# Half of an output projection moved beside the attention, and probabilities flipped bank by bank

## The chip, the cores and the metric

The kernel runs on one core of one Trainium2 chip. The time is what the device takes for one execution, in microseconds (us); the figure of a kernel is the median over several runs. TensorE (PE in the profile) does the matrix products, VectorE (DVE), ScalarE (ACT) and GpSimd (POOL) the rest, SyncE (SP) issues the DMAs. Each engine works through its own instructions in a fixed order.

## The reference, cut to what matters

One Conformer-like block with D = 1024 and 512 positions, in float32:

```python
x = x + 0.5 * swiglu(rmsnorm(x, ffn1_norm), ffn1_w_gate, ffn1_w_up, ffn1_w_down)
proj = rmsnorm(x, mix_norm) @ w_in
out_a = chunked_relbias_attention(qa, ka, va, a_rel_bias)   # 8 heads of 64, chunks of 64, bias by distance
out_b = mla_attention(...)                                  # 8 heads of 96 (64 + 32 rotary), values of 64
x = x + jnp.concatenate([out_a, out_b], axis=-1) @ w_out
x = x + 0.5 * swiglu(rmsnorm(x, ffn2_norm), ffn2_w_gate, ffn2_w_up, ffn2_w_down)
x = rmsnorm(x, final_norm)
```

Both attentions are causal by blocks, so of the 4 x 4 blocks of 128 positions of a head only the ten on and below the diagonal are computed.

## The kernel before, in words

x stands transposed, as eight tiles `x[k]` of 128 features by 512 positions. Every matrix product is done in three passes on split numbers: a value is a rounded high part (a cast on ACT) and a low part (value minus high part, on DVE or POOL); `mm3` (L145 to L149) issues high x high (L147), the second pass L148 and the third L149. Weights come by `wunit` (L136 to L144): one DMA of 512 KB into one of four `raw` buffers, a cast to `whi` on ACT (L142), a subtraction to `wlo` on POOL (L143); `whi` and `wlo` have four buffers each.

The stages are: first feed-forward (gate and up products `gu`, down products `dn`), input projections and latents, 16 attention heads, output projection, second feed-forward, last norm. Heads 0 to 7 are those of A, heads 8 to 15 those of B. A loop over `it` from -2 to 16 (L569 to L578) lets four steps overlap: `flip(it)`, `softmax(it + 1)`, `front(it + 2)`, `values(it - 1)`.

- `front` turns queries and keys by TensorE transposes (tile `tr`, L457) and splits them on ACT (L461) and DVE (L462).
- `softmax` makes scores of four query blocks into `s3`, `s2` and the two halves of `s01`. Per block one DVE operation adds bias or mask and takes the row's minimum (L522, `mn`), ACT takes the exponential and the sum (L524), DVE the reciprocal (L525), POOL the product (L526). The probabilities lie in `pa` and `pb`, two of the four `raw` buffers.
- `flip` transposes the ten blocks of probabilities by TensorE (L542) into three PSUM banks `t0`, `t1`, `t2`, query block by query block, and copies them out as high parts on ACT (L547: PAh, PBh, in `whi` buffers) and low parts on DVE (L548: PAl, PBl, in `wlo` buffers).
- `values` multiplies with V into the bank `pv`; two heads share one, and after the second one ACT (L562) and DVE (L563) split it into AH[c], AL[c] (`xh`, `xl`), c = 0 to 3 for A and 4 to 7 for B.

The attention's eight PSUM banks are: 2 for `s`, 2 for `tr`, 3 for `t`, 1 for `pv`; in-projections before it use them in two groups of four (`bank`). The output projection (L589 to L599) then takes for each of eight tiles `dt` one `wunit` of `w_out[dt]`, 24 matmuls over c = 0 to 7 into one of seven banks of a new pool, adds the sum into `x[dt]` on DVE (L595) and prepares the second feed-forward: x2h on ACT (L596), x2l on DVE (L597), squares on ACT and their sum on POOL (`add_square`, L110).

The order in which an engine's instructions stand is not the source's: the framework's scheduler simulates the program's timing as it records it and sorts each engine's instructions by that. A tile that takes over a buffer waits for the last use of the buffer before.

## Time and profile before

| | us |
|---|---|
| median of 3 runs | 996.52 (996.40 to 996.64) |
| the profiled execution | 997.57 |
| its span | 995.8 |
| TensorE busy | 975.5 (98%) |
| POOL busy | 579.6 (58%) |
| ACT busy | 391.9 (39%) |
| DVE busy | 390.5 (39%) |
| attention up to the first `wo` matmul, starts at 482 | 579.30 |
| output projection up to the first second-stage `gu` matmul | 622.83 |

The last two rows are places on the span's clock. Busy times overlap; TensorE is the only engine that is busy nearly always. An idle engine other than it costs nothing by itself; an idle TensorE does, as no later stage is limited by anything else.

### The profile page before, as it was taken

The numbers are of one execution on the slowest core, as the hardware profiler recorded it, in microseconds if no ns is written. First come the engines' busy times: TensorE is split into PE (matmuls) and PEld (weight loads), VectorE is DVE, ScalarE is ACT, GpSimd is POOL, SyncE is SP. The second block draws the span as 40 slices with busy tenths as digits, with TensorE's granted clock in tenths as the row PEclk, the third lists the DMA queues.
The fourth block names the chain that finished last, engine by engine and source line by source line (L and its number), as shares of the span: only waits on it lengthen the run. The fifth ranks groups of instructions, "written<-read, shape, count | busy, mean of one in ns | idle before, by whom it ended". The sixth has DMA issues, their size and how long they took to land.

```text
span 995.8 us, 12076 instructions
## 1 busy us (share of the span) xinstructions
PE 975.5 (98%) x4579; PEld 812.1 (82%) x4579; DVE 390.5 (39%) x684; ACT 391.9 (39%) x661; POOL 579.6 (58%) x424
## 2 busy tenths in 40 slices
PE   9999999999999999898999999999999999999996
PEld 6888888888888889786778978888888888888886
DVE  7533333333121233866788845143333333200002
ACT  7533323232222236563778853343233232322321
POOL 4776666765555530385445567587666667645541
PEclk9999999999999999999999999999999999999998
DMA  6432223233233242220110062323322232333302
GB/s 233 145 109 86 102 89 106 85 106 95 83 102 93 89 141 75 85 64 1 32 33 2 1 212 88 103 86 106 102 88 99 93 104 80 101 96 95 101 16 85
DMA packets 29146, 89.90 MB, mean 90 GB/s; under 512 B 3488, under 2 KB 5664, under 8 KB 29088
## 3 DMA queue, kind: packets, MB, share of 16 engines
q1 hardware_dynamic: 28224, 88.34, 27.6%
q8 instruction: 36, 0.59, 0.2%
q10 hardware_dynamic: 864, 0.79, 0.2%
q14 instruction: 22, 0.18, 0.1%
HBM read 87.02 MB, written 2.10 MB: 89 GB/s over the span
## 4 chain that ended last, share of the span: by engine, by line
PE 89%; DVE 4%; ACT 3%; POOL 2%; issue 1%; DMA 1%; SPq 0%; POOLq 0%; ACTq 0%; DVEq 0%
PE gu L147 15%; PE gu L149 15%; PE gu L148 15%; PE dn L147 8%; PE dn L149 8%; PE dn L148 8%; PE pj L149 2%; PE pj L147 2%; PE pj L148 2%; PE wo L147 1%; PE wo L149 1%; PE wo L148 1%; PE t L542 1%; PE s L147 1%; PE tr L457 1%
## 5 line engine op out<-in xcount | busy, mean ns | idle before, releaser
L143 POOL TENSOR_TENSOR wlo<-raw,whi 128x1024 fp32r<-128x1024 f32 x138 | 324.2, 2350 | 153.3 <-ACT whi L142 152.5
L142 ACT CAST whi<-raw 128x1024 fp32r<-128x1024 f32 (+2 forms) x159 | 162.4, 1022 | 447.7 <-PE gu L148 244.8
L147 PE MATMUL gu<-x2h,whi 128*128 128x512 f32 x352 | 136.9, 389 | 0.0
L148 PE MATMUL gu<-x2l,whi 128*128 128x512 f32 x352 | 136.8, 389 | 0.0
L149 PE MATMUL gu<-x2h,wlo 128*128 128x512 f32 x352 | 136.8, 389 | 0.0
L148 PE MATMUL gu<-xl,whi 128*128 128x512 f32 x320 | 124.5, 389 | 0.0
L147 PE MATMUL gu<-xh,whi 128*128 128x512 f32 x320 | 124.5, 389 | 0.0
L149 PE MATMUL gu<-xh,wlo 128*128 128x512 f32 x320 | 124.5, 389 | 0.0
L162 POOL TENSOR_TENSOR us<-us,gs 128x512 f32<-128x512 f32 x44 | 57.6, 1310 | 108.7 <-DVE us L160 107.2
L161 DVE SCALAR_TENSOR_TENSOR gs<-th,gs 128x512 f32<-128x512 f32 x44 | 91.1, 2074 | 31.8 <-ACT th L159 31.8
L158 DVE TENSOR_TENSOR gs<-gu,rs 128x512 f32<-128x512 f32 x44 | 30.4, 691 | 175.9 <-PE gu L149 168.7
L191 DVE SCALAR_TENSOR_TENSOR x<-dn,x 128x512 f32<-128x512 f32 (+1 forms) x17 | 11.2, 660 | 193.9 <-PE dn L149 193.9
L148 PEld LDWEIGHTS gu<-x2l,whi 128*128 128x128 f32 x352 | 66.1, 188 | 13.8
L149 PEld LDWEIGHTS gu<-x2h,wlo 128*128 128x128 f32 x352 | 66.1, 188 | 13.8
L147 PEld LDWEIGHTS gu<-x2h,whi 128*128 128x128 f32 x352 | 66.1, 188 | 13.6
L149 PEld LDWEIGHTS gu<-xh,wlo 128*128 128x128 f32 x320 | 60.1, 188 | 12.6
L147 PEld LDWEIGHTS gu<-xh,whi 128*128 128x128 f32 x320 | 60.1, 188 | 12.5
L148 PEld LDWEIGHTS gu<-xl,whi 128*128 128x128 f32 x320 | 60.1, 188 | 12.3
L147 PE MATMUL dn<-h1h,whi 128*128 128x512 f32 x176 | 68.5, 389 | 0.0
L148 PE MATMUL dn<-h1l,whi 128*128 128x512 f32 x176 | 68.5, 389 | 0.0
L149 PE MATMUL dn<-h1h,wlo 128*128 128x512 f32 x176 | 68.5, 389 | 0.0
L160 DVE SCALAR_TENSOR_TENSOR us<-gu,rs 128x512 f32<-128x512 f32 x44 | 30.4, 690 | 64.9 <-PE gu L149 64.9
(327 smaller groups left out, 1864.5 us busy)
## 6 DMA issues: line engine op xcount, KB each, us to landing
raw<-in_gu SPq DMA_DIRECT2D x84, 512.0 KB, 3.6
raw<-in_dn SPq DMA_DIRECT2D x32, 512.0 KB, 3.5
raw<-in_dn SPq DMA_DIRECT2D x16, 384.0 KB, 3.1
raw<-in_w_in SPq DMA_DIRECT2D x12, 512.0 KB, 3.4
raw<-in_w_out SPq DMA_DIRECT2D x8, 512.0 KB, 4.3
x<-in_xT SPq DMA_DIRECT2D x8, 256.0 KB, 5.4
raw<-in_gu SPq DMA_DIRECT2D x8, 256.0 KB, 5.4
bias<-in_bias_tab SPq DMA_DIRECT2D x8, 256.0 KB, 2.7
```

Source lines behind the costliest of these rows:

```text
L142: act.copy(hi[:, :n], raw[:, :n])
L143: (lo_on or pool).tensor_tensor(out=lo[:, :n], in0=raw[:, :n], in1=hi[:, :n].bitcast(F32), op=ALU.subtract)
L147: pe.matmul(out, lhsT=ah, rhs=bh, start=start, stop=False)
L148: pe.matmul(out, lhsT=ah, rhs=bl, start=False, stop=False)
L149: pe.matmul(out, lhsT=al, rhs=bh, start=False, stop=stop)
L158: dve.tensor_tensor(out=gs, in0=gup[0], in1=rs, op=ALU.mult)
L160: dve.scalar_tensor_tensor(out=us, in0=gup[1], scalar=0.5, in1=rs, op0=ALU.mult, op1=ALU.mult)
L161: dve.scalar_tensor_tensor(out=gs, in0=th, scalar=1.0, in1=gs, op0=ALU.add, op1=ALU.mult)
L162: pool.tensor_tensor(out=us, in0=us, in1=gs, op=ALU.mult)
L191: dve.scalar_tensor_tensor(out=x[dt][:, h], in0=pt[:, h], scalar=0.5, in1=x[dt][:, h], op0=ALU.mult, op1=ALU.add)
L457: pe.transpose(pt[0:src(t).shape[1], t * P:(t + 1) * P], src(t), ident)
L542: pe.transpose(tt[:, o + i * P:o + (i + 1) * P], pi[i][:, j * P:(j + 1) * P], ident)
```

## The change

`w_out` is laid out anew on the host side of the inputs: as (half, pair of tiles, 128, 1024), so that one 512 KB unit holds four of the eight c for two tiles `dt`.

- The A half (c = 0 to 3): `weights_o` loads one unit in each of the loop's rounds 8 to 11, casts it on ACT (L576 after) and subtracts on POOL (L577 after); the results stay in SBUF, the first three in the place of A's split V (`vAh`, `vAl`), the fourth in that of A's keys (`kA`). `out_a(dt)`, in rounds 9 to 16, does 12 matmuls into the PSUM bank `pj` and adds the sum into `x[dt]` on DVE.
- The B half (c = 4 to 7): in round 16 a `wunit` and `out_b(0)`, also in bank `pj`, around the values of the last head; the other seven tiles in the loop behind, 12 matmuls each, with three more `wunit`s.
- `flip` goes probability column block by column block: three groups of 3, 3 and 4 transposes, each in one of two banks `t` (the third is now `pj`), each copied out behind it (L544 transposes, L546 and L547 copies after).

```diff
@@ -304,11 +304,11 @@
             pool.tensor_tensor(out=dst[:, :, :, 16:32], in0=a, in1=b, op=ALU.add)
 
         with tc.tile_pool(name="ps2", bufs=1, space=PSUM, reuse_waits="tile") as ps:
-            NB = {"s": 2, "tr": 2, "t": 3, "pv": 1}
+            NB = {"s": 2, "tr": 2, "t": 2, "pv": 1, "pj": 1}
 
             def bank(group, i, name):
 
-                tag = (("s",) * NB["s"] + ("tr",) * NB["tr"], ("t",) * NB["t"] + ("pv",) * NB["pv"])[group][i]
+                tag = (("s", "s", "tr", "tr"), ("t", "t", "pj", "pv"))[group][i]
                 return ps.tile([P, 512], F32, tag=tag, name=name, bufs=NB[tag])
 
             def in_proj(off, n, group):
@@ -528,24 +528,23 @@
 
             def flip(pi):
 
-                t0 = ps.tile([P, 512], F32, tag="t", name="t0", bufs=NB["t"])
-                t1 = ps.tile([P, 512], F32, tag="t", name="t1", bufs=NB["t"])
-                t2 = ps.tile([P, 512], F32, tag="t", name="t2", bufs=NB["t"])
                 PAh = wpool.tile([P, 1024], F32R, tag="whi", name="PAh")
                 PAl = wpool.tile([P, 1024], F32R, tag="wlo", name="PAl")
                 PBh = wpool.tile([P, 1024], F32R, tag="whi", name="PBh")
                 PBl = wpool.tile([P, 1024], F32R, tag="wlo", name="PBl")
-                where = {0: (t0, 0), 1: (t1, -128), 2: (t2, -256), 3: (t2, 0)}
-                for i in (3, 2, 1, 0):
-                    for j in range(i + 1):
-                        tt, o = where[j]
-                        pe.transpose(tt[:, o + i * P:o + (i + 1) * P], pi[i][:, j * P:(j + 1) * P], ident)
                 for hl in (PBh, PBl):
                     pool.memset(hl[:, 256:384].bitcast(F32), 0.0)
-                for h_, l_, src in ((PBh[:, 384:512], PBl[:, 384:512], t2[:, 384:512]), (PBh[:, 0:256], PBl[:, 0:256], t2[:, 0:256]),
-                                    (PAh[:, 512:896], PAl[:, 512:896], t1[:, 0:384]), (PAh[:, 0:512], PAl[:, 0:512], t0)):
-                    act.copy(h_, src)
-                    dve.tensor_tensor(out=l_, in0=src, in1=h_.bitcast(F32), op=ALU.subtract)
+
+                for keys, copies in ((((3, 0), (2, -256)), ((PBh[:, 384:512], PBl[:, 384:512], 384, 512), (PBh[:, 0:256], PBl[:, 0:256], 0, 256))),
+                                     (((1, -128),), ((PAh[:, 512:896], PAl[:, 512:896], 0, 384),)),
+                                     (((0, 0),), ((PAh[:, 0:512], PAl[:, 0:512], 0, 512),))):
+                    tt = ps.tile([P, 512], F32, tag="t", name="tp", bufs=NB["t"])
+                    for j, o in keys:
+                        for i in range(NT - 1, j - 1, -1):
+                            pe.transpose(tt[:, o + i * P:o + (i + 1) * P], pi[i][:, j * P:(j + 1) * P], ident)
+                    for h_, l_, c0, c1 in copies:
+                        act.copy(h_, tt[:, c0:c1])
+                        dve.tensor_tensor(out=l_, in0=tt[:, c0:c1], in1=h_.bitcast(F32), op=ALU.subtract)
                 return [(PAh[:, 0:512], PAl[:, 0:512], 0), (PAh[:, 512:896], PAl[:, 512:896], 128),
                         (PBh[:, 0:256], PBl[:, 0:256], 256), (PBh[:, 256:512], PBl[:, 256:512], 256)]
 
@@ -562,6 +561,40 @@
                     act.copy(AH[c], pv)
                     dve.tensor_tensor(out=AL[c], in0=pv, in1=AH[c].bitcast(F32), op=ALU.subtract)
 
+            W = {}
+
+
+            def weights_o(i):
+
+                if i == 0:
+                    W["oh"] = mp.tile([P, 3, 1024], F32R, tag="vAh", name="woh")
+                    W["ol"] = mp.tile([P, 3, 1024], F32R, tag="vAl", name="wol")
+                    W["o3"] = mp.tile([P, 2, 1024], F32R, tag="kA", name="wo3")
+                hi, lo = (W["oh"][:, i], W["ol"][:, i]) if i < 3 else (W["o3"][:, 0], W["o3"][:, 1])
+                raw = wraw.tile([P, 1024], F32, tag="raw", name="raw")
+                nc.sync.dma_start(out=raw, in_=w_out[0, i])
+                act.copy(hi, raw)
+                pool.tensor_tensor(out=lo, in0=raw, in1=hi.bitcast(F32), op=ALU.subtract)
+                W["o", i] = hi, lo
+
+            def out_a(dt):
+                hi, lo = W["o", dt // 2]
+                pt = ps.tile([P, 512], F32, tag="pj", name="woa", bufs=NB["pj"])
+                for c in range(4):
+                    cc = slice((dt % 2) * 512 + c * P, (dt % 2) * 512 + (c + 1) * P)
+                    mm3(pt, hi[:, cc], lo[:, cc], AH[c], AL[c], c == 0, c == 3)
+                dve.tensor_tensor(out=x[dt], in0=pt, in1=x[dt], op=ALU.add)
+
+            def out_b(dt, c0, c1):
+                if c0 == 4:
+                    W["b", dt] = ps.tile([P, 512], F32, tag="pj", name="wob", bufs=NB["pj"])
+                pt, (hi, lo) = W["b", dt], W["wb"]
+                for c in range(c0, c1):
+                    cc = slice(dt * 512 + (c - 4) * P, dt * 512 + (c - 3) * P)
+                    mm3(pt, hi[:, cc], lo[:, cc], AH[c], AL[c], c == 4, c == KD - 1)
+                if c1 == KD:
+                    dve.tensor_tensor(out=x[dt], in0=pt, in1=x[dt], op=ALU.add)
+
 
             shared["V"] = values_proj()
             n = 2 * NH
@@ -574,8 +607,16 @@
                         prob[it + 1] = softmax(*qk.pop(it + 1))
                     if it + 2 < n:
                         qk[it + 2] = front(it + 2)
+                if it == n:
+                    W["wb"] = wunit(w_out[1, 0], 1024)
+                    out_b(0, 4, KD - 1)
                 if it >= 1:
                     values(it - 1, seg.pop(it - 1))
+                if NH <= it < NH + 4:
+                    weights_o(it - NH)
+                if NH < it <= 2 * NH:
+                    out_a(it - NH - 1)
+            out_b(0, KD - 1, KD)
 
 
     with tc.tile_pool(name="h2", bufs=1, side="left", reuse_waits="tile") as hp, \
@@ -587,12 +628,14 @@
         H = list(zip(HH, HL))
         H += [(XH[k], XL[k]) for k in range(KD)]
         for dt in range(KD):
-            hi, lo = wunit(w_out[dt], 1024)
-            pt = ps.tile([P, S], F32, tag="mm", name="wo")
-            for c in range(KD):
-                cc = slice(c * P, (c + 1) * P)
-                mm3(pt, hi[:, cc], lo[:, cc], AH[c], AL[c], c == 0, c == KD - 1)
-            dve.tensor_tensor(out=x[dt], in0=pt, in1=x[dt], op=ALU.add)
+            if dt % 2 == 0:
+                hi, lo = W["wb"] if dt == 0 else wunit(w_out[1, dt // 2], 1024)
+            if dt > 0:
+                pt = ps.tile([P, S], F32, tag="mm", name="wo")
+                for c in range(4, KD):
+                    cc = slice((dt % 2) * 512 + (c - 4) * P, (dt % 2) * 512 + (c - 3) * P)
+                    mm3(pt, hi[:, cc], lo[:, cc], AH[c], AL[c], c == 4, c == KD - 1)
+                dve.tensor_tensor(out=x[dt], in0=pt, in1=x[dt], op=ALU.add)
             act.activation(X2H[dt], x[dt], AF.Copy, scale=g(C_FFN2 + dt))
             dve.scalar_tensor_tensor(out=X2L[dt], in0=x[dt], scalar=g(C_FFN2 + dt), in1=X2H[dt].bitcast(F32),
                                      op0=ALU.mult, op1=ALU.subtract)
@@ -718,8 +761,9 @@
     out["w_in"] = np.concatenate([_kxm(p, KD, p.shape[1]).reshape(P, -1) for p in parts], axis=1)
     out["w_uq"] = np.stack([_kxm(a["b_w_uq"][:, 384 * s:384 * s + 384], 2, 384).reshape(P, -1) for s in range(2)])
     out["w_ukv"] = a["b_w_ukv"]
-    wo = a["w_out"].reshape(KD, P, KD, P).transpose(2, 1, 0, 3)
-    out["w_out"] = wo.reshape(KD, P, KD * P)
+
+    wo = a["w_out"].reshape(2, 4, P, 4, 2, P).transpose(0, 3, 2, 4, 1, 5)
+    out["w_out"] = wo.reshape(2, 4, P, KD * P)
     return {k: np.ascontiguousarray(v) for k, v in out.items()}
 
 
```

How the change moves instructions, at three places.

TensorE, between two A heads; `t_`/`tp` are the banks of transposed probabilities, `pv_3764` the values of head 0 and 1, `s3_3808` the first scores of the head after next. Before:

```order
L148 MATMUL pv_3764<-PAl_3622,VAh_3417 128x512
L149 MATMUL pv_3764<-PAh_3621,VAl_3418 128x512
L147 MATMUL pv_3764<-PAh_3621,VAh_3417 128x384
L148 MATMUL pv_3764<-PAl_3622,VAh_3417 128x384
L149 MATMUL pv_3764<-PAh_3621,VAl_3418 128x384
L147 MATMUL pv_3764<-PBh_3623,VAh_3417 128x256
L148 MATMUL pv_3764<-PBl_3624,VAh_3417 128x256
L149 MATMUL pv_3764<-PBh_3623,VAl_3418 128x256
L147 MATMUL pv_3764<-PBh_3623,VAh_3417 128x256
L148 MATMUL pv_3764<-PBl_3624,VAh_3417 128x256
L149 MATMUL pv_3764<-PBh_3623,VAl_3418 128x256
L147 MATMUL s3_3808<-xh5_86,xh4_85 128x512
```

After:

```order
L544 MATMUL tp_3704<-ident_123,pa_3645 128x128 x3
L147 MATMUL s01_3731<-xh5_86,xh4_85 128x256
L148 MATMUL s01_3731<-xl5_94,xh4_85 128x256
L149 MATMUL s01_3731<-xh5_86,xl4_93 128x256
L147 MATMUL pv_3764<-PAh_3618,VAh_3417 128x512
L147 MATMUL s3_3808<-xh5_86,xh4_85 128x512
L148 MATMUL s3_3808<-xl5_94,xh4_85 128x512
L149 MATMUL s3_3808<-xh5_86,xl4_93 128x512
L544 MATMUL tp_3712<-ident_123,pa_3645 128x128 x2
L544 MATMUL tp_3712<-ident_123,pb_3646 128x128
L148 MATMUL pv_3764<-PAl_3619,VAh_3417 128x512
L149 MATMUL pv_3764<-PAh_3618,VAl_3418 128x512
```

The scores `s3_3808` stood behind all the values of head 0; now they and the head's second group of transposes stand after the first matmul of these values.

ACT, where the first weights of the A half come (`woh_4411`); `PAh_4414` and `PBh_4416` before, `PAh_4418` and `PBh_4420` after, are the copies of head 9's transposes; pa and pb are exponentials. Before, and then after:

```order
L524 ACTIVATE pa_4438,sm_4441<-pa_4438,mn_4440 128x384
L524 ACTIVATE pb_4439,sm_4441<-pb_4439,mn_4440 128x256
L547 CAST PAh_4414<-t0_4411 128x512
L461 ACTIVATE qh_4564<-tr_4566,nq_2589 96x512
L461 ACTIVATE kst_4185<-tr_4573,col_97 64x512
L524 ACTIVATE pb_4439,sm_4441<-pb_4439,mn_4440 128x128
L547 CAST PAh_4414<-t1_4412 128x384
```

```order
L524 ACTIVATE pa_4445,sm_4448<-pa_4445,mn_4447 128x384
L546 CAST PBh_4420<-tp_4424 128x256
L576 CAST woh_4411<-raw_4414 128x1024
L546 CAST PAh_4418<-tp_4432 128x384
L546 CAST PAh_4418<-tp_4438 128x512
L524 ACTIVATE pb_4446,sm_4448<-pb_4446,mn_4447 128x256
L546 CAST PBh_4529<-tp_4533 128x128
```

The cast of the weights stands between head 9's first and second group of copies.

ACT at the end of the attention; `PAh_4947`, `PBh_4949` before and `PAh_5047`, `PBh_5049` after are copies of the last head's transposes, `xh7_88` the split of the last values. Before, and then after:

```order
L547 CAST PAh_4947<-t1_4945 128x384
L547 CAST PAh_4947<-t0_4944 128x512
L142 CAST whi_5052<-raw_5050 128x1024
L547 CAST PBh_4949<-t2_4946 128x128
L142 CAST whi_5087<-raw_5085 128x1024
L547 CAST PBh_4949<-t2_4946 128x256
L142 CAST whi_5124<-raw_5122 128x1024
L562 CAST xh7_88<-pv_4971 128x512
```

```order
L546 CAST PBh_5049<-tp_5053 128x128
L524 ACTIVATE pb_4985,sm_4987<-pb_4985,mn_4986 128x128
L546 CAST PAh_5047<-tp_5061 128x384
L546 CAST PBh_5049<-tp_5053 128x256
L142 CAST whi_5103<-raw_5101 128x1024
L142 CAST whi_5225<-raw_5223 128x1024
L546 CAST PAh_5047<-tp_5067 128x512
L142 CAST whi_5269<-raw_5267 128x1024
L561 CAST xh7_88<-pv_5074 128x512
```

Both large copies of the last head stood ahead of every cast of weights; now one stands behind two casts, and three casts stand ahead of `xh7_88`.

TensorE at the same place: the end of the last head's values (`pv_4971` before, `pv_5074` after) and what follows them. Before:

```order
L147 MATMUL pv_4971<-PBh_4949,VBh_2566 128x256
L148 MATMUL pv_4971<-PBl_4950,VBh_2566 128x256
L149 MATMUL pv_4971<-PBh_4949,VBl_2568 128x256
L147 MATMUL wo_5056<-xh0_81,whi_5052 128x512
L148 MATMUL wo_5056<-xl0_89,whi_5052 128x512
L149 MATMUL wo_5056<-xh0_81,wlo_5053 128x512
L147 MATMUL wo_5056<-xh1_82,whi_5052 128x512
L148 MATMUL wo_5056<-xl1_90,whi_5052 128x512
```

After, the last group of transposes and what follows, and then the end of the values' successor `wob_5107`:

```order
L544 MATMUL tp_5067<-ident_123,pa_4984 128x128 x2
L544 MATMUL tp_5067<-ident_123,pb_4985 128x128 x2
L147 MATMUL wob_5107<-xh4_85,whi_5103 128x512
L148 MATMUL wob_5107<-xl4_93,whi_5103 128x512
L147 MATMUL pv_5074<-PAh_5047,VBh_2566 128x512
L148 MATMUL pv_5074<-PAl_5048,VBh_2566 128x512
L149 MATMUL pv_5074<-PAh_5047,VBl_2568 128x512
```

```order
L149 MATMUL wob_5107<-xh6_87,wlo_5104 128x512
L147 MATMUL wob_5107<-xh7_88,whi_5103 128x512
L148 MATMUL wob_5107<-xl7_96,whi_5103 128x512
L149 MATMUL wob_5107<-xh7_88,wlo_5104 128x512
L147 MATMUL woa_5131<-xh0_81,wo3_4413 128x512
L148 MATMUL woa_5131<-xl0_89,wo3_4413 128x512
L149 MATMUL woa_5131<-xh0_81,wo3_4413 128x512
```

The first sum of the projection began with the six finished c of A and B; now its B half begins with two matmuls ahead of the last values and goes on behind them, and the last block of A, `woa_5131`, stands behind that.

## Rows read from the trace of the kernel before

**Rows 1.** Busy time by stretch: range, length, engines with (instructions), PEclk, DMA share, GB/s.

```profile
482.00:539.00 57.00, 55.74 (x347) 44.04 (x346) 48.85 (x172) 44.11 (x130) 29.49 (x61) 1.00 0.11 29
539.00:572.00 33.00, 33.00 (x232) 30.52 (x232) 28.98 (x106) 27.71 (x81) 19.25 (x39) 1.00 0.01 1
572.00:580.00 8.00, 7.31 (x43) 5.74 (x43) 3.99 (x10) 6.63 (x14) 3.61 (x3) 1.00 0.76 264
580.00:623.00 43.00, 43.00 (x191) 35.63 (x190) 22.61 (x15) 16.71 (x24) 33.44 (x18) 1.00 0.40 128
```

**Rows 2.** Waits of TensorE: line, released by; us in total, times, longest.

```profile
PE s L147 <- DVE mn L522: 0.8, 2, 0.4
```

**Rows 3.** TensorE row by row, A heads: start, us of one, operation, count, [idle before].

```profile
485.69 0.60 PE L457 MATMUL tr<-ident,qA 128*128 128x128 f32 x4
486.22 0.50 PE L147 MATMUL s<-xh,xh 64*128 64x512 f32 x1
486.56 0.39 PE L148 MATMUL s<-xl,xh 64*128 64x512 f32 x1
486.79 0.39 PE L149 MATMUL s<-xh,xl 64*128 64x512 f32 x1
487.12 0.66 PE L457 MATMUL tr<-ident,kA 128*128 128x128 f32 x4
...
491.22 0.48 PE L148 MATMUL pv<-PAl,VAh 128*128 128x512 f32 x1
491.54 0.40 PE L149 MATMUL pv<-PAh,VAl 128*128 128x512 f32 x1
```

**Rows 4.** TensorE row by row, the last heads, the projection's start and end.

```profile
571.50 0.49 PE L542 MATMUL t<-ident,pa 128*128 128x128 f32 x3
571.75 0.36 PE L148 MATMUL pv<-PBl,VBh 128*128 128x256 f32 x1
...
573.07 0.44 PE L542 MATMUL t<-ident,pa 128*128 128x128 f32 x2 [0.15 <-DVE PAl L548]
...
574.10 0.50 PE L147 MATMUL pv<-PAh,VBh 128*128 128x512 f32 x1 [0.15 <-DVE xl L563]
...
576.46 0.40 PE L147 MATMUL pv<-PAh,VBh 128*128 128x512 f32 x1
...
578.15 0.38 PE L147 MATMUL pv<-PBh,VBh 128*128 128x256 f32 x1 [0.30 <-ACT PBh L547]
...
579.30 0.40 PE L147 MATMUL wo<-xh,whi 128*128 128x512 f32 x1
...
622.83 0.39 PE L147 MATMUL gu<-x2h,whi 128*128 128x512 f32 x1
```

**Rows 5.** Instructions grouped by form, 479 to 623: count, busy us, mean ns, idle.

```profile
L143 POOL TENSOR_TENSOR wlo<-raw,whi 128x1024 fp32r<-128x1024 f32 x11 | 26.2, 2398 | 12.4 <-ACT whi L142 12.4
...
L142 ACT CAST whi<-raw 128x1024 fp32r<-128x1024 f32 x12 | 12.6, 1050 | 27.4 <-PE wo L148 16.1 <-POOL ssum L110 6.5 <-issue 3.2
...
L524 ACT ACTIVATE pa<-pa,mn 128x512 f32<-128x512 f32 x15 | 10.9, 729 | 0.5 <-DVE mn L522 0.4
...
L548 DVE TENSOR_TENSOR PAl<-t,PAh 128x512 fp32r<-128x512 f32 x16 | 10.9, 682 | 0.7 <-ACT PAh L547 0.6
...
L547 ACT CAST PAh<-t 128x512 fp32r<-128x512 f32 x16 | 9.3, 584 | 3.3 <-PE t L542 3.1
...
L110 POOL TENSOR_TENSOR ssum<-ssum,sq 128x512 f32<-128x512 f32 x6 | 10.5, 1753 | 0.0
...
L522 DVE CUSTOM_DVE_ANT_0 pa<-s,mask 128x512 f32<-128x512 f32 x8 | 5.5, 685 | 0.8 <-POOL pa L526 0.4 <-PE t L542 0.2
```

**Rows 6.** DVE row by row, the first addition into x.

```profile
584.95 0.69 DVE L595 TENSOR_TENSOR x<-wo,x 128x512 f32<-128x512 f32 x1 [4.14 <-PE wo L149]
```

**Rows 7.** SP row by row: the eight loads of output weights.

```profile
571.70 15.09 SPq L139 DMA_DIRECT2D raw<-in_w_out  x8
```

**Rows 8.** The loads of w_out: from issue to landing.

```profile
DMA to landing us min/median/max: 3.5/4.3/4.4
```

## The prediction

> **What bounds the kernel now.** I read the busy times by stretch first [rows 1], then the waits of TensorE [rows 2], then TensorE row by row at the two places the change touches, the A heads and the end of the attention [rows 3, 4], and last what ACT, POOL and the DMAs do there [rows 5 to 8]. The reader is to see in [rows 1] that TensorE is the bound of every stretch: 55.74 of 57.00 us while the A heads run, 33.00 of 33.00 in the B heads up to 572, 7.31 of 8.00 in the last head, 43.00 of 43.00 in the output projection. The granted clock is 1.00 in all of them, so no term below is one of the clock. A change that keeps all matmuls and only moves them can win just what TensorE idles, and can lose by new waits.
>
> What it idles: in the A heads [rows 2] name 0.8 us of score matmuls waiting for `mn`; at the end [rows 4] show 0.15, 0.15 and 0.30. Busy time hides more, as its ends are modelled; the distances between starts show it. In [rows 3] the first 64-row score matmul (A's heads are 64 wide) starts 0.53 after four transposes, which take 0.44; the second one 0.34 after the first and the third 0.23 after that, which is the plain distance for 512 columns; the next 128-row operation starts 0.33 after the third. One excursion into 64 rows costs 0.09 + 0.11 + 0.10 = 0.3. At the end [rows 4], from the issue of head 14's last transposes (571.50) to the first `wo` matmul (579.30) 7.80 us pass. The work in them: 3 transposes at 0.11, 5 matmuls of 256 columns at 0.118, 10 transposes, and two heads' values at 1.91 each (574.10 to 576.46 is 2.36, less three transposes between and 0.11 on entry); 0.33 + 0.59 + 1.09 + 3.82 = 5.83. So TensorE loses 2.0 us there, the named waits and what the distances add to them.
>
> **The change part by part.**
>
> *Totals.* 192 matmuls of 512 columns at 0.227 (43.53 us between 579.30 and 622.83 [rows 4]), eight 512 KB loads, eight casts of 1.05 on ACT and eight subtractions of 2.40 on POOL stay [rows 5]. Eight additions into x of 0.69 on DVE [rows 6] are new; DVE has 28.98 busy of 33.00 in the B heads and gets 22 us more time there. 96 of the matmuls leave the end for the B heads. That moves 21.8 us of TensorE work and saves none of it: where they are put, TensorE was busy 33.00 of 33.00. On SP four loads move ahead into a stretch where nothing else is issued; on POOL four subtractions of 2.40 go between normalisations (19.25 busy of 33.00), and each can hold the next one back by 2.4, about what the 12 matmuls of a block (2.7) cover: nothing in the sum, part of the middle's upper bound.
>
> *A heads: flips bank by bank.* The order puts s3 of a head earlier, so that the copies which give `mn` are done when s2 needs a bank: I take both waits for `mn` away, -0.8. One of 25 excursions into 64 rows goes, -0.3. Transposes stand in 25 groups instead of 34 before the first values of B; the second matmul behind such a group starts up to 0.1 late (491.54 in [rows 3]), and most of that is given back before it (571.75 in [rows 4] comes 0.25 after three transposes, which take 0.33), so 9 x 0.04 = -0.4. Against it: two banks for three groups, so the second group of a head must find the third group of the head before copied out, a cast of 0.58 and a subtraction of 0.68 [rows 5]. Meanwhile TensorE has 3 transposes, s2, s01, one pv matmul and s3: 0.33 + 0.53 + 0.35 + 0.23 + 0.69 = 2.1. Two copies and their hand-overs, 1.3 to 1.6, fit in 2.1 unless an exponential (0.73) and more stand ahead of them; I take one miss in three of 8 heads at 0.1, +0.3. Sum -1.2; bounds -2.5 (every idle of A that the distances between starts show beyond the excursions, 2.1, and the groups) and +1.5 (a miss of 0.2 in each of 8 heads, nothing gained).
>
> *B heads: the first weights.* The load for the first half block takes a buffer that head 8's probabilities leave after their last transpose; the eight loads of before land after 3.5 to 4.4 [rows 8]. ACT's order puts the cast of these weights ahead of the copies of head 9's second and third group, so those copies wait for a DMA, and the values of head 9 and the next first group for the copies. The 12 matmuls of the first block cover 2.7 us of values work around it, the rest stays: about 0.3 before the block's first matmul and 0.55 behind it (the copy's 0.58), +0.8. The three later weights have a block of 12 matmuls (2.7) in front and are covered. Between 0 (covered by blocks) and +2.5 (each of four at 0.6).
>
> *The end.* This is where the largest term is. I count from the end of head 14's last transposes, where the first load of B's half can go (before: the issue at 571.70 [rows 7]). Loads take 3.5 to 4.4, and ACT's order is now: cast first weights, cast second weights, copy of head 15's third group, cast third weights, xh of head 15. Before, head 15's big copies stood ahead of all the weights.
>  - TensorE has 0.8 of head 14's work, 0.33 + 0.33 of transposes, 1.91 of values and 0.44 of transposes: 3.8. The first weights are landed at 3.8 and cast at 4.8: 1.0 lost in front of the two `wob` matmuls, which take it to 5.3.
>  - The second weights land at 4.9 and are cast at 5.95, the copy of the third group follows at 6.6: 1.3 lost, and 0.5 more until its low part (0.68 on DVE behind the 0.58) for the second matmul.
>  - Values end near 9.1, seven `wob` matmuls (1.6) follow to 10.7. The third weights have taken the buffer of head 15, freed near 4.5, landed by 8.9 and keep ACT until 9.9; then xh 0.59, xl 0.69, 11.2: 0.5 lost before the last three. Before, 21 matmuls of `wo` on the seven finished pairs of heads (4.8) covered this pair of copies.
>  - `wob` done, the last A block wants the same bank: it waits for the addition into x. In [rows 6] that starts 0.43 after the issue of the last matmul of its sum (579.30 + 23 x 0.227 = 584.52), 0.20 more than the matmul's own place, and takes 0.69; with a hand-over back 0.95. Before, `wo` had seven banks.
>  Sum 1.0 + 1.3 + 0.5 + 0.5 + 0.95 = 4.25, with 0.25 of small hand-overs 4.5. Before it was 2.0, so +2.5. Bounds: +1 (loads at 3.5 and the last A block no wait) and +4.5 (loads at 4.4 and later buffers).
> [...]
>
> *Behind it.* POOL has 33.44 of 43.00 in the projection [rows 1], as 2.40 and 1.75 run per block [rows 5]; per pair of blocks it will be 2.40 + 2 x 1.75 = 5.9 against 2 x 12 matmuls = 5.45. It lags by 0.45 per pair, 1.8 in four, and x's sum of squares is wanted only after a first gate matmul group, some 20 us later. I cost it at nothing; without that cover it would be 1.8.
>
> **Sum.** -1.2 + 0.8 + 2.5 = +2.1. The profiled execution took 997.57 (span 995.8 and 1.8 around it), so 999.7 of its kind; the median shown is 996.52, 1.05 lower. 996.52 + 2.1 = 998.6.
>
> **The rivals.**
> 1. *The regimes fill each other.* Blocks of independent matmuls between the heads of B take every wait there: the 2.0 at the end, because a block stands beside the last heads, and A's 2.1, and the idle of the middle: -2.0 to -4.5, about 993.3. For it: the last A block needs nothing new from head 15. Against it: in the order it stands behind the `wob` matmuls that wait for head 15, and [rows 1] leave nothing to fill in B's middle. The Trainium skill (Perfetto Trace Analysis, Optimization Strategy) says that kernels whose most contended engine changes over time may gain by interleaving these stretches. The trace does not show that condition: TensorE is the bound in all of [rows 1].
> 2. *Two banks are too few.* Slower: the second group waits in every head. It decides from the point where cast and subtraction, with what stands ahead of them on ACT and DVE, take longer than the 2.1 us of TensorE work between. With one exponential (0.73) and one score reduction (0.68) ahead they take 1.3 + 1.4 = 2.7, so 0.6 in each of 16 heads, 9.6; in half of them 4.8. With the +2.5 of the end that is 1004 to 1009. Against it: in ACT's order at the end one exponential at most stands directly ahead of a copy. The Trainium skill (Perfetto Trace Analysis, Matmuls) wants independent groups to rotate through different PSUM banks so that one's evacuation lies beside the next one's matmuls; by it, a third bank given away is a loss.
> 3. *Nothing comes of it.* The end costs +1, as loads land in 3.5 and copies squeeze in, and A gives -1: 996.5. For it: 2.0 of the end are lost already. Against it: the new order of ACT's casts.
>
> **How the numbers follow.** The forecast 0.45, rival 1 0.24, rival 2 0.11, rival 3 0.20. About 0.2% (2 us) is what a measurement of this kernel can tell from no change, so faster means under 994.5 and slower over 998.5. Faster: rival 1 but its smallest gains, 0.23. Same: rival 3 with 0.20, and 0.19 of the forecast's own lower half: 0.39, those gains in it. Slower: the rest, 0.38. The forecast's own range is 997 to 1001. For 8 in 10 the range goes down into rival 1, to 993.8, and up by the bounds of the middle and the end, to 1002.2.
>
> **What would show it.** Right, step by step: the waits for `mn` gone; a wait of a values matmul near the first `woa` matmul for the copies L546 of head 9; at the end TensorE waits for ACT's casts L142 before the first `wob`, for L546 before head 15's values, for xl before the last `wob`, and for the DVE addition before the last `woa` block. From the end of head 14's transposes to the first gate matmul TensorE would lose 4 to 5 us. Wrong: if that is under 3, if a transposition group of A waits for L547 in most heads, or if the B heads up to the last one grow by clearly more or less than the 19 us of seven blocks.

## The result, and the profile after

The changed kernel takes 1000.56 us (median of 7 executions, 999.26 to 1005.2) against 996.52 (7, 995.45 to 997.76): ratio 1.0053, 95% interval 1.004 to 1.0065, so about 5 us slower by the ratio and 4.0 by the two medians. Its profiled execution took 1000.56 with a span of 998.8, 3.0 more than the span before.

Busy time by stretch in the changed kernel, in the same stretches as [rows 1]:

```profile
482.00:539.00 57.00, 55.29 (x335) 43.99 (x334) 46.80 (x169) 43.87 (x125) 28.47 (x60) 1.00 0.10 29
539.00:572.00 33.00, 32.72 (x204) 28.90 (x203) 24.29 (x74) 23.83 (x60) 21.09 (x28) 1.00 0.21 65
572.00:580.00 8.00, 8.00 (x52) 7.09 (x51) 5.02 (x15) 4.28 (x13) 3.53 (x6) 1.00 0.00 0
580.00:623.00 43.00, 40.65 (x206) 33.58 (x205) 23.70 (x51) 22.21 (x44) 25.37 (x24) 1.00 0.36 123
```

The stretches no longer hold the same work, so they tell only where TensorE idles now: 1.7 us in the A heads and 2.4 in the last one, where the last B heads and the projection stand. To compare like with like, I take the time from the last in-projection matmul (`pj`) to the first gate matmul behind the projection (`gu`), which holds the same matrix products in every kernel here: 141.6 us before (481.23 to 622.83) and 145.2 after (481.02 to 626.26), 3.65 more. From that gate matmul to the last instruction of TensorE both take 366 us. What TensorE loses in that time against the plain distances of its matmuls (0.227, 0.174, 0.118 and 0.109 us for 512, 384, 256 and 128 columns) is 12.3 us before and 15.9 after: up to the first values of B 9.3 and 10.7, behind it 3.0 and 5.2.

The waits of TensorE in the changed kernel from 482 us on (us in total, times, longest; one of 0.2 is left out), which answer to [rows 2]:

```profile
PE tp L544 <- DVE PAl L547: 1.5, 3, 1.0
PE woa L147 <- DVE x L596: 0.8, 1, 0.8
PE pv L147 <- ACT PAh L546: 0.7, 1, 0.7
PE tr L457 <- DVE xl L462: 0.5, 1, 0.5
PE pv L147 <- DVE xl L562: 0.4, 1, 0.4
```

The 0.8 of `mn` are gone, and all five rows are new or larger than before. Row by row, TensorE in the first A heads:

```profile
486.34 0.39 PE L149 MATMUL s<-xh,xl 64*128 64x512 f32 x1
487.74 0.44 PE L544 MATMUL tp<-ident,pa 128*128 128x128 f32 x2 [1.01 <-DVE PAl L547]
...
502.74 0.64 PE L457 MATMUL tr<-ident,kpe 128*96 128x128 f32 x4 [0.55 <-DVE xl L462]
```

and DVE at the first of them:

```profile
485.92 0.47 DVE L449 SCALAR_TENSOR_TENSOR VAl<-pj,rtok,VAh 128x256 fp32r<-128x256 f32 x1
486.31 0.15 DVE L525 RECIPROCAL sm<-sm 128x1 f32<-128x1 f32 x1
486.38 0.83 DVE L482 TENSOR_SCALAR bias<-bias 128x512 f32<-128x512 f32 x1
487.14 0.54 DVE L547 TENSOR_TENSOR PAl<-tp,PAh 128x384 fp32r<-128x384 f32 x1
```

The third group of head 0 needs a bank, and of the two the one of the second group comes free first. Its high part was cast at 485.00, but the low part (487.14) stands behind a split of V, a reciprocal and the negation of a bias, 1.4 us of other work. The kernels below with a third bank for these transposes do not show this wait. The last wait shown, 0.55 before the first transposes for B (502.74), is for a split on DVE (L462).

TensorE at the end of the attention, answering to [rows 4]:

```profile
593.51 0.44 PE L544 MATMUL tp<-ident,pa 128*128 128x128 f32 x2 [0.24 <-DVE PAl L547]
594.41 0.47 PE L147 MATMUL pv<-PAh,VBh 128*128 128x512 f32 x1 [0.35 <-DVE xl L562]
597.06 0.50 PE L147 MATMUL wob<-xh,whi 128*128 128x512 f32 x1
597.40 0.39 PE L148 MATMUL wob<-xl,whi 128*128 128x512 f32 x1
598.49 0.49 PE L147 MATMUL pv<-PAh,VBh 128*128 128x512 f32 x1 [0.71 <-ACT PAh L546]
599.22 0.50 PE L148 MATMUL pv<-PAl,VBh 128*128 128x512 f32 x1 [0.23 <-DVE PAl L547]
604.34 0.50 PE L147 MATMUL woa<-xh,wo 128*128 128x512 f32 x1 [0.78 <-DVE x L596]
626.26 0.39 PE L147 MATMUL gu<-x2h,whi 128*128 128x512 f32 x1
```

and ACT there:

```profile
595.96 1.99 ACT L142 CAST whi<-raw 128x1024 fp32r<-128x1024 f32 x2 [1.09 <-PE pv L149]
597.86 0.58 ACT L546 CAST PAh<-tp 128x512 fp32r<-128x512 f32 x1
```

The copy for the last head's values (597.86) stands behind two casts of weights, and TensorE waits for it, for its low part, and for the addition into x before the last A block: 1.09 instead of 0.23 from 597.40 to 598.49, 0.73 to 599.22, 1.18 from 603.16 to 604.34. From 604.34 to 626.26 the last 96 matmuls take 21.9 us, their plain 21.8: POOL's lag costs nothing.

### The profile page after: what moved, and what is told of

It reads as the page before. It is cut to its first block, busy times and chain, and to the rows that moved or that the text cites. A ratio compares the mean times of both kernels' runs of the same rounds, so it can differ in the third digit from the quotient of the medians.

```text
span 998.8 us, 12078 instructions
## 1 busy us (share of the span) xinstructions
PE 977.9 (98%) x4579; PEld 815.0 (82%) x4579; DVE 390.9 (39%) x692; ACT 394.3 (39%) x661; POOL 578.6 (58%) x424
## 4 chain that ended last, share of the span: by engine, by line
PE 93%; DVE 3%; issue 1%; ACT 1%; DMA 1%; POOL 0%; SPq 0%; POOLq 0%; DVEq 0%
PE gu L147 15%; PE gu L148 15%; PE gu L149 15%; PE dn L147 8%; PE dn L149 8%; PE dn L148 8%; PE pj L149 3%; PE pj L147 3%; PE pj L148 3%; PE tp L544 2%; PE s L147 1%; PE tr L457 1%; PE pv L147 1%; PE gu L232 1%; PE pv L148 1%
## 5 line engine op out<-in xcount | busy, mean ns | idle before, releaser
L143 POOL TENSOR_TENSOR wlo<-raw,whi 128x1024 fp32r<-128x1024 f32 x134 | 314.9, 2351 | 143.4 <-ACT whi L142 142.6
L142 ACT CAST whi<-raw 128x1024 fp32r<-128x1024 f32 (+2 forms) x155 | 158.1, 1020 | 425.8 <-PE gu L148 242.5
L149 PEld LDWEIGHTS gu<-x2h,wlo 128*128 128x128 f32 x352 | 66.1, 188 | 13.7
L147 PEld LDWEIGHTS gu<-xh,whi 128*128 128x128 f32 x320 | 60.1, 188 | 12.3
L526 POOL TENSOR_TENSOR pa<-pa,sm 128x512 f32<-128x512 f32 (+1 forms) x32 | 29.9, 942 | 47.0 <-DVE sm L525 42.9
```

Of the source, the lines that this page charges most:

```text
L142: act.copy(hi[:, :n], raw[:, :n])
L143: (lo_on or pool).tensor_tensor(out=lo[:, :n], in0=raw[:, :n], in1=hi[:, :n].bitcast(F32), op=ALU.subtract)
L147: pe.matmul(out, lhsT=ah, rhs=bh, start=start, stop=False)
L149: pe.matmul(out, lhsT=al, rhs=bh, start=False, stop=stop)
L526: pool.tensor_tensor(out=pi[i], in0=pi[i], in1=sm[:, i:i + 1].broadcast_to([P, (i + 1) * P]), op=ALU.mult)
```

## The experiments

The ratios are to the kernel before, run on the same chip. "pj to gu" is the time just described, from each kernel's profiled execution.

| kernel | median us | ratio (95%) | pj to gu |
|---|---|---|---|
| before, by group of runs | 995.35 to 996.52 | 1 | 141.6 |
| changed | 1000.56 | 1.0053 (1.004 to 1.0065) | 145.2 |
| changed, again | 1001.77 | 1.0049 (1.0032 to 1.0066) | 145.1 |
| new flips alone, two banks | 1004.52 | 1.0088 (1.0075 to 1.0101) | 151.6 |
| new flips alone, three banks | 995.73 | 0.9999 (0.999 to 1.0008) | 140.6 |
| changed, first B half no special case | 1000.88 | 1.0044 (1.0032 to 1.0056) | 145.1 |
| the same, three shared banks | 991.47 | 0.9954 (0.9942 to 0.9965) | 136.6 |
| the move alone, old flips, three shared banks | 994.62 | 0.998 (0.9971 to 0.9989) | 139.8 |
| changed, pj lent to all A heads | 995.89 | 0.9996 (0.9988 to 1.0005) | 141.7 |
| changed, pj lent to the first A head | 998.24 | 1.0028 (1.0016 to 1.004) | 144.1 |
| changed, three shared banks | 990.74 | 0.9943 (0.9931 to 0.9954) | 136.6 |

**The flips alone, over two banks and over three.** Both have the new `flip` and the old projection; the first has

```diff
-            NB = {"s": 2, "tr": 2, "t": 3, "pv": 1}
+            NB = {"s": 2, "tr": 2, "t": 2, "pv": 1, "pj": 1}
```

with `pj` used by the in-projections only, the second keeps the three banks of before.

> The new flips alone, over two banks, with the projection of before. By the distances of the profile after, TensorE loses 1.8 us more than before in the first three A heads (1.1 of it before the third group of transposes of the first head, 0.6 before the transposes of kpe) and 1.7 more at the end. Theory 1 (the loss in A comes from the flips over two banks, not from the moved projection): 1.5 to 2.0 us slower than the kernel before, ratio 1.0015 to 1.002, with a wait of about 1.0 us of transposes for a low part of the copies in the first head. Theory 2 (the flips are free, and the moved work makes all of the loss): ratio 0.9995 to 1.0005 and no such wait.

> The new flips, with three banks as before, and the projection of before. Theory 1a (it is the number of banks): the wait of 1.0 us in the first head is gone, the A heads within 0.4 us of the kernel before, ratio 0.9995 to 1.0005. Theory 1b (it is the order of the flips by banks, whatever their number): a loss of 1.5 to 2.0 us in the first heads as with two banks, ratio 1.0015 to 1.002.

Over two banks the loss is 8.8 us, far more than either theory gave, with the wait of 1.0 us of theory 1. Part of what is above it is the clock. Busy time of TensorE by stretch in this kernel (length, busy, granted clock, DMA), and rows of it:

```profile
482.00:486.00 4.00, 4.00 (x28) 1.00 0.27 70
486.00:490.00 4.00, 3.00 (x15) 0.92 0.18 66
490.00:494.00 4.00, 4.00 (x11) 0.50 0.00 0
494.00:498.00 4.00, 4.00 (x21) 0.72 0.00 2
498.00:510.00 12.00, 11.45 (x68) 1.00 0.17 46
584.00:590.00 6.00, 5.16 (x19) 0.72 0.89 309
```

```profile
487.19 0.44 PE L544 MATMUL tp<-ident,pa 128*128 128x128 f32 x2 [1.00 <-DVE PAl L547]
...
490.89 0.63 PE L148 MATMUL s<-xl,xh 64*128 64x512 f32 x1
491.32 0.62 PE L149 MATMUL s<-xh,xl 64*128 64x512 f32 x1
...
584.63 0.53 PE L147 MATMUL pv<-PAh,VBh 128*128 128x512 f32 x1 [1.92 <-ACT PAh L546]
```

Some 2 us behind the wait in the first head the clock falls to its lower level (0.50, 1.2 GHz): 490.89 to 491.32 is 0.43 us for 512 columns, plain 0.227. It comes back near 496, after about 7 us (the 0.92, 0.50 and 0.72 of three stretches of 4 us). The order of TensorE up to there is that of the changed kernel, whose profile lost 10.7 us before B's values; here it is 13.7, so this stretch costs 2.9. The second such stretch follows the wait at 584.63 and costs about 1.5: from 585.36 to the first `wo` matmul at 588.52 pass 3.16 us, plain 1.68. The other part is not the clock. This profile is 10.0 longer than before from pj to gu, 4.3 up to B's first values and 5.7 behind them; beside the 4.4 of the clock and the 1.4 that the changed kernel loses in A, too, some 4.2 are lost by new waits in the B heads, the longest of them the 1.92 at 584.63, which neither theory counted.

With three banks the wait is gone and the ratio is 1: theory 1a. But that is two changes that cancel, so the theory, which had the A heads within 0.4 us of before, met its ratio by luck. In its profile TensorE loses 6.4 us before B's values instead of 9.3, so the flips by banks gain 3.0 in A; behind it the loss is 5.0 instead of 3.0, because the last head's copy now stands behind the casts of weights there, too:

```profile
576.67 0.50 PE L147 MATMUL pv<-PAh,VBh 128*128 128x512 f32 x1 [1.79 <-ACT PAh L546]
577.40 0.50 PE L148 MATMUL pv<-PAl,VBh 128*128 128x512 f32 x1 [0.22 <-DVE PAl L547]
```

**No special case for the first B half, with the bank of its own and with three shared banks.** The first drops `out_b` and lets the loop behind take all eight tiles:

```diff
                     W["wb"] = wunit(w_out[1, 0], 1024)
-                    out_b(0, 4, KD - 1)
...
-            out_b(0, KD - 1, KD)
```

The second also gives the bank back (`woa` in the tag `t`, three banks as before).

> As the changed kernel, but the B half of the first tile is no special case: it goes into the loop behind with the other seven, in a bank of its own. Theory 1 (the last A block waits behind the B half for the shared bank, 0.95, and where it stands it covers no wait of the last head, 1.4): the end loses about 1.7 us instead of 3.7, so 1.5 to 2.0 us faster than the changed kernel, ratio to the kernel before about 1.003 if that of the changed kernel is 1.005. Rival (the casts of weights ahead of the last copies set the end, whatever stands in TensorE's queue): only the 0.95 is gained, ratio about 1.0043.

> As the one without the special case, and the bank of the projection is given back: three banks shared by the transposed probabilities and the A blocks. Theory 1: the first heads lose no more than before (1.8 us back), and the last two A blocks stand in front of the last head's values, so the end loses under 1.5 us: ratio to the kernel before 0.998 to 1.0005. Rival (a block that holds one of the three banks for 2.7 us and an addition makes the flips wait, 0.4 us or more in each of the eight B heads): ratio 1.002 or more, with waits of transposes for x additions.

The first gains nothing that can be told from the changed kernel: its rival came nearer in the ratio. The wait for the addition is gone, but the last values wait longer, as there are fewer matmuls before them, and a stretch at the lower clock follows:

```profile
599.01 0.49 PE L147 MATMUL pv<-PAh,VBh 128*128 128x512 f32 x1 [1.45 <-ACT PAh L546]
599.73 0.50 PE L148 MATMUL pv<-PAl,VBh 128*128 128x512 f32 x1 [0.23 <-DVE PAl L547]
...
602.61 0.63 PE L148 MATMUL wo<-xl,whi 128*128 128x512 f32 x1
603.03 0.63 PE L149 MATMUL wo<-xh,wlo 128*128 128x512 f32 x1
```

From 600.67 to 604.25 the distances are those of the lower clock, worth 1.5 us; without it the expected gain would have been there in this execution. So it does not settle how much the special case costs by itself. With three shared banks the result is 0.9954, faster than theory 1 had it: TensorE loses 6.3 before B's values and 1.0 behind. The rival is out: no transposition waits for an addition.

**The whole change, with only the bank given back.** Special case included:

```diff
-            NB = {"s": 2, "tr": 2, "t": 2, "pv": 1, "pj": 1}
+            NB = {"s": 2, "tr": 2, "t": 3, "pv": 1}
...
-                pt = ps.tile([P, 512], F32, tag="pj", name="woa", bufs=NB["pj"])
+                pt = ps.tile([P, 512], F32, tag="t", name="woa", bufs=NB["t"])
...
-                    W["b", dt] = ps.tile([P, 512], F32, tag="pj", name="wob", bufs=NB["pj"])
+                    W["b", dt] = ps.tile([P, 512], F32, tag="t", name="wob", bufs=NB["t"])
```

> The whole change, special case included, with only the bank given back: three banks shared by transposed probabilities, A blocks and the first B half. Theory 1 (the bank of its own is what made the change slow): as without the special case, ratio 0.995 to 0.9965, no wait of the last A block for the addition into x. Rival (the special case costs its 1 us and more at the end also with three banks): ratio 0.997 to 0.999.

990.74 us, ratio 0.9943: the best of all, 5.7 us faster than before, 11 faster than the changed kernel of the same group, by where two tiles lie. The special case costs nothing here. TensorE and ACT at the last values:

```profile
587.87 0.48 PE L147 MATMUL woa<-xh,wo 128*128 128x512 f32 x1
...
590.71 0.39 PE L147 MATMUL wob<-xh,whi 128*128 128x512 f32 x1
590.94 0.39 PE L148 MATMUL wob<-xl,whi 128*128 128x512 f32 x1
591.16 0.39 PE L147 MATMUL pv<-PAh,VBh 128*128 128x512 f32 x1
```

```profile
587.04 2.00 ACT L142 CAST whi<-raw 128x1024 fp32r<-128x1024 f32 x2 [0.30 <-ACT PBh L546]
588.95 0.57 ACT L546 CAST PAh<-tp 128x512 fp32r<-128x512 f32 x1
```

ACT's order is the same as in the changed kernel: the copy behind two casts. But a whole A block of 12 matmuls (587.87 to 590.71) now stands in front of the values, and nothing waits. The blocks come later here, since they take turns with the transposes for the banks, so that three of the eight stand behind head 14's last transposes, where the changed kernel has one. That the sharing is what delays them is read from the orders; no run isolates it.

**The move alone.** Old flips over `t0`, `t1`, `t2`, the blocks in the same three banks, no special case.

> The move alone: the flips of before over t0, t1, t2, the A half beside the B heads in banks of the same three, no special case for the first B half. Theory 1 (the moved blocks take TensorE's waits in the last heads, the flips by banks those of A): the A heads lose as before (9.3 us with the changes into 64 rows), B about 1 instead of 3.0: ratio 0.9975 to 0.9985. Rival (a flip that wants all three banks at once waits for a block that holds one): ratio 1.001 or more, waits of transposes for x additions in most B heads.

0.998, as theory 1 has it: 9.2 lost before B's values and 1.4 behind. The waits for `mn` are there as in [rows 2]:

```profile
PE s L147 <- DVE mn L522: 1.0, 3, 0.4
```

**The bank lent to the A heads.** It is idle there, so the third group of each flip takes it, in all A heads (`lend` is `it < NH`) or in the first alone (`it < 1`):

```diff
-                    tt = ps.tile([P, 512], F32, tag="t", name="tp", bufs=NB["t"])
+                    tg = "pj" if lend and keys[0][0] == 0 else "t"
+                    tt = ps.tile([P, 512], F32, tag=tg, name="tp", bufs=NB[tg])
```

> The changed kernel, but in the A heads the third group of each flip goes into the bank pj, which is idle there. Theory 1 (A's loss is the missing third bank): the wait of 1.0 us in the first head is gone, A loses 6.3 to 6.7 instead of 10.7, B stays at 5.2: 4 us and more faster than the changed kernel, ratio 0.999 to 1.001. Rival (what counts is the order of the flips at the first heads, or the kpe transposes): less than 1.5 us faster, ratio 1.003 or more.

Lent to all A heads: 0.9996, 6.9 lost before B's values (10.7 in the changed kernel) and 5.6 behind it. The rest of the loss at the end is untouched, the waits of the changed kernel's end row by row (its L546 and L547 are L547 and L548 here):

```profile
PE pv L147 <- ACT PAh L547: 0.9, 2, 0.7
...
PE woa L147 <- DVE x L597: 0.8, 1, 0.8
PE tp L545 <- DVE PAl L548: 0.5, 2, 0.2
```

**The spread of the changed kernel.** Of its 13 timed executions in two groups of runs seven lie between 998.93 and 1000.56 with a mean clock of 0.992 to 0.994, six between 1003.13 and 1005.2 with 0.988 to 0.991. The 0.988 stands in no profile here; 0.991 alone tells little, as the profile of the move alone has it with 1.00 all through the attention and the projection.

> The changed kernel, unaltered, a second time, beside the others of this group. Theory 1 (waits of TensorE of 1 us and more are followed in some executions by a stretch at half the granted clock, as the flips over two banks alone showed at 490 to 496): ratio 1.004 to 1.0065 again, and the executions spread by 4 us or more, the longer ones with the lower mean clock; a profile in the upper half shows a clock of about 0.5 to 0.7 behind the wait of 1.0 us in the first head or behind those at the end. Rival (the stages of the profile say all): every execution near +3.5 us, ratio 1.003 to 1.004, whatever the clock.

> The changed kernel, with the bank pj lent to the third group of transposes of the very first A head only; behind that head TensorE's order is that of the changed kernel but for two rows. The executions of the changed kernel fall into two groups, near 999.4 and near 1003.6 us. Theory 1 (the upper group is the one in which TensorE's clock is halved for some us behind the wait of 1.0 us in the first head): the wait is gone and with it the upper group: executions between 996.5 and 999.5, median 3 us or more under the changed kernel, ratio 1.001 to 1.003. Rival (the two groups come from elsewhere, as from the waits at the end): the same two groups, each about 1 us lower, median about 1000.5, ratio 1.0035 to 1.0045.

> The changed kernel, unaltered, one execution more. If it falls into the upper group (near 1003.6 us), theory 1 expects in the stretch of some 10 us behind the wait of the first head a granted clock well below 1.00 and 1.00 behind the waits at the end; the rival expects 1.00 there and a lower clock elsewhere. In the lower group (near 999.4 us) both expect 1.00 in both places.

With the bank lent to the first head alone, all eight executions lie between 997.59 and 1000.59 and none near 1003; ratio 1.0028. pj to gu is 1.0 shorter than in the changed kernel, but the ratio fell by 0.0021 to 0.0025, 2.1 to 2.5 us. So in these eight executions the upper group went with one wait of 1.0 us, which is for theory 1, though two of the eight lie above the 999.5 that it gave. It is not proof: the six upper executions are of other groups of runs, those of the repetition on another chip. One more execution of the changed kernel came out at 1001.77, between the groups, with a clock of 1.00 behind the wait, and decides nothing. The three profiles of the changed kernel (998.93, 1000.56, 1001.77) agree in pj to gu (145.1, 145.2, 145.2); they differ ahead of it, where nothing was changed: the last `pj` matmul starts at 479.12, 481.02 and 482.37. None of them was caught at the lower clock behind the wait. That the clock falls there is shown directly only in the kernel with the flips alone.

## Why the prediction was right, and where it was not

The time was put at 998.6, 993.8 to 1002.2; it is 1000.56, and slower as forecast, though the chances had "same" (0.39) level with "slower" (0.38), and by the medians the change is +4.0 where the sum had +2.1. By the terms of the sum that is partly luck. In the profile the A heads cost +1.4, the middle +0.1, the end +2.0 and what is behind it +0.2; A was 2.6 worse than its term, and the middle and the end, 1.2 better than theirs, hid part of it.

- *The end, +2.5.* The mechanism is right and the size a little high. Against 2.0 before, TensorE loses 3.9 from head 14's last transposes (591.51) to the last A block (604.34): +2.0. Of the five pieces, 1.3 in front of the last values measured 0.87, 0.5 for the low part 0.50, and the last A block's 0.95 measured 0.95. The 1.0 in front of the first `wob` is 0.20, since TensorE came there later (0.40 and 0.51 lost in front of 593.51 and 594.41) and the weights landed after 3.4; their cast then stood until 595.96, for a values matmul of head 14 that used the buffer, not for the load. The 0.5 in front of the last three `wob` is 0.06: the third weights were cast from 600.52 on, and the seven `wob` matmuls before covered both copies. The rest is some 0.1 at each start behind a wait.
- *The middle, +0.8.* 0.45 lost at the first block for the copy of head 9 (546.11 to 546.79), by a group of transposes that wants its bank and not by a values matmul, and nothing else of that size; the total behind A is +0.1 up to the last heads. The price of the load ahead of the copies was set too high.
- *A heads, -1.2.* The step that failed. Measured +1.4. The waits for `mn` went as said. What I had as "one miss in three of 8 heads at 0.1" was one miss of 1.0 in the first head: I weighed the copies' own 1.3 to 1.6 us against TensorE's 2.1, but not what stands ahead of the low part on DVE, which is 1.4 there; nor which of the two banks the third group takes. And with the bank the gain that the flips bring was lost, too: three banks show 6.4 instead of the 9.3 of before, two show 10.7. Part of this is the wait of 0.55 before B's first transposes, which stays when the bank is lent to the first head alone and is gone wherever all A heads have three. Part is in excursions into 64 rows: 25 before, 24 in the changed kernel, 20 with three banks, at the 0.3 of [rows 3]. The Trainium skill (TensorEngine Tiling (Array Packing), Key Properties) says that a change of the tiling mode drains TensorE; [rows 3] fit that, with 0.3 for a change there and back, if matmuls of 64 rows are such a mode, which no row shows.
- *No term of the clock.* The rows of before had 1.00 throughout these stretches, and I took it for granted that new waits of 1 us would not change it. In the flips alone over two banks they did, for 4.4 us. For the changed kernel it is not shown: its median execution is the profiled one, at 1.00, so the 4.0 of the medians have nothing of the clock in them. Its lower group lies 3.2 above the mean of before (999.7 against 996.5), near the 3.65 of the profile, its upper group 7.3; if the lower clock makes the upper group, it is the difference between the profile and the 5 of the ratio.
- *Rival 2* (two banks are too few) happened in kind, in one head and not in all, with 1.0 and not 0.6 a head. The rule of the Trainium skill that it named (Perfetto Trace Analysis, Matmuls: rotate through different banks) is borne out: the same flips take 995.73 over three banks and 1004.52 over two, some 4.4 of that by the lower clock. *Rival 1* (the regimes fill each other) I put down for the order, in which the last block stands behind the `wob` matmuls, and for [rows 1], which "leave nothing to fill in B's middle". The middle has nothing to fill, but the end has, and where the banks put a block in front of the last values, it fills it. With three banks and old flips the move takes the loss behind A from 3.0 to 1.4, with new flips from 5.0 to 1.0. So what the Trainium skill (Perfetto Trace Analysis, Optimization Strategy) says of interleaving stretches pays for this kernel, too, in the last microseconds of its attention, though TensorE stays the bound there (7.31 of 8.00 in [rows 1]). What kept that from the changed kernel is that the bank of its own released the blocks too early for the end and took the third bank from the flips.

What stays open: how often and why the lower clock follows a wait of 1 us in one execution and not in the next, and whether it makes the upper group of the changed kernel.

## What to carry to other kernels

A bank of its own for independent filler work is paid by the group that it is taken from; before giving it, let the filler take turns in the banks that are there. When two buffers replace three, price the copy-out by everything that stands ahead of it on its engine, in the first round above all, where other stages' leftovers lie. And keep independent matmuls for the very end of a latency-bound stretch: the same casts stood ahead of the same copy, and one block of 12 matmuls in front of the values made it cost nothing.

## What of the hardware was not expected

A wait of TensorE of 1.0 us amid busy work was followed, some 2 us later, by about 7 us at a granted clock of 0.50 in one profile (512 columns in 0.43 us instead of 0.227), and not in four other profiles of kernels with the same wait at the same place; waits of 1.5 and 1.9 us at the end were followed by it in two kernels, one of 1.8 us in a third was not. Such a stretch cost 1.5 to 2.9 us, as much as the wait before it or more in two of the three.
